# Retention heads with stored block sums and the next values' first product ahead of the scores; MLP down sums accumulated in SBUF; background jobs further apart

## The chip, the cores and the metric

The kernel runs on one core of one Trainium2 chip. The metric is device time in microseconds. Engine names are those of the profile: PE is TensorE's array, PEld its weight loads, DVE VectorE, ACT ScalarE, POOL GpSimd, SP SyncE, which issues most DMAs.

## The reference

One layer of a hybrid block for 512 tokens of width 1024, in float32. Two branches work on the normalized input; a gated mix of them goes through w_out, and an MLP follows.

```python
xn = rmsnorm(x, n_mix_pre)
qa, ka, va, za, beta_logit, a_dt, qb, kb, vb, gb, gate_a, gate_b = split(xn @ w_in)
# Branch A: causal convolution, silu, gated delta rule in chunks of 64, 8 heads
oa = rmsnorm(chunk_gated_delta_rule(qa, ka, va, beta, g), norm_a) * silu(za)
ya = oa @ w_br_a
# Branch B: 4 retention heads, keys of 256, values of 512
qb, kb = rotary(qb), rotary(kb) * 256 ** -0.5
ob = chunk_retention(qb, kb, vb)
ob = rmsnorm(ob, norm_b) * silu(gb)
yb = ob @ w_br_b
mix = (sigmoid(gate_a) * ya + sigmoid(gate_b) * yb) @ w_out
x = x + rmsnorm(mix, n_mix_post)
ff = square(relu(rmsnorm(x, n_mlp_pre) @ w_up)) @ w_down        # d_ff = 4096
out = x + rmsnorm(ff, n_mlp_post)
```

## The kernel before

**Products.** Every float32 matrix is split into a high part (`whi`, made by ACT at L148) and the rest (`wlo`, made by DVE at L149), and a product is three matmuls: high by high, high by low, low by high (`mm3` at L93 to L95; in block products the loop at L322). A weight tile is 128 x 1024 float32, 512 KB. It is loaded by SP into a buffer named `raw` (L103 straight from a weight matrix, L197 for a block), split, and used by 12 matmuls of 512 columns.

**Seven products.** The large products are done by blocks: two by two blocks of the activations and of the weights, with sums of blocks, need seven block products for eight. They are called "11", "12", "22", "s1" to "s4". The activation sums are made on chip. The weight sums come in two ways. Class `BlockSums` stores them in DRAM: a copy DRAM to DRAM on SP's queue (`copy_block`, L169) puts a block into a DRAM tile `sums`, and an accumulating DMA on POOL's queue (`add_block`, L135) adds another block to it. Where sums are not stored, DVE adds raw tiles (`plus`, in Branch B at L1651).

**The pace of the background.** Copies and adds are jobs of two lists, `trickle` and `later_adds`. `pace` is called at each load as the program is built: if the kernel's own clock, a count of matmul columns, has passed `queued`, one job is put right behind that load, and `queued` grows by `JOB_US` = 7.8 (none in the model's time 860 to 985). Where a sum is wanted before its jobs were placed, `raw` places them at once. There are 140 jobs.

**Branch B.** Head h runs as follows: query and key projections, rotary (L1543 to L1549; the key's high and low parts `kr` at L1548 and L1549), scores in four tiles of 512, 384, 256 and 256 columns, times a decay mask into `sc` (L1583), then values and gates by seven products (`seven`, called by `values_and_gates`), the outputs and their norm. The branch product with w_br_b of head h-1 is a Python generator, `branch_seven`; it is started within head h, behind the keys: "11" and "12" run, then `yield`; then the scores; then "s2", "s1", "s3", "s4", "22". Its activations are `og` (features of the head before), its sums of them `osum` (L1628), made from `upper`; its results are added into `acc` at L1658. The PSUM pool psx has three banks `dl` and one `tr`, the pool psm four banks `mm`.

**MLP.** Four groups: an up projection of 1024 columns (`hn` by w_up, relu and square, rows `r` at L1922), then `seven_down`, a block product in the order "11", "12", "s2", "s1", "s3", "s4", "22" (in the last group "s1" ahead of "s2"). Its results add up in `facc`.

**Order.** Each engine's instructions stand in the order that a list scheduler gives them from program order and `tc.high_priority(n)`: a larger n stands earlier. The block products' matmuls are kept in program order. A load stands on SP when the buffer that it fills has been handed out; there are two raw pools of two buffers in Branch B.

Of the kernel before, what the change touches and what calls it, by code (L numbers as in the profile page):

```python
# [10 lines left out]
F32 = mybir.dt.float32  # L11
# [8 lines left out]
P = 128  # L20
# [8 lines left out]
JOBS_FROM, JOB_US = 70.0, 7.8  # L29
# [34 lines left out]
def hybrid_block_kernel(ctx: ExitStack, tc: tile.TileContext, a: dict, out: bass.AP):  # L64
# [90 lines left out]
    class BlockSums:  # L155


        def __init__(self, src, c1, c2, tag, full=True, kts=4):
# [4 lines left out]
            self.made = (2, 1, 3, 0) if full else (2, 0)  # L163
            self.t = {i: dr.tile([P, kts, 512], F32, tag=f"{tag}{i}", name="sums", bufs=1) for i in self.made}
# [18 lines left out]
        def raw(self, i, ks):  # L183
            while any(job[0] is self for job in trickle):
                copy_block()
            while any(dst is t for dst, *_ in later_adds for t in self.parts):
                add_block()
            return block_raw(self.t[i - 1][:, 2 * ks : 2 * ks + 2, :])
# [4 lines left out]
    def block_raw(block):  # L193
# [8 lines left out]
    ga_sums = BlockSums(w_in, OFF_GA, OFF_GA + 512, "ga", False)  # L202
    vg_sums, br_sums = [], []
    for h in range(4):
        vg_sums.append(BlockSums(w_in, OFF_VB + h * 512, OFF_GB + h * 512, f"vg{h}", False))
# [45 lines left out]
    def seven(src, c1, c2, sums, product, temp, out):  # L251
# [1257 lines left out]
    with tc.tile_pool(name="pb", bufs=1) as pb_:  # L1509
# [11 lines left out]
        def values_and_gates(sums, c1, c2, g, out1, out2):  # L1521

            def out(th, ch, ps, u=None, op=None):
                for t in range(2):
                    row = 2 * th + t
                    if ch:
                        nc.vector.tensor_tensor(g[:, row, :], ps[t], u[t], op)
# [8 lines left out]
            seven(w_in, c1, c2, sums, token_product(quarters), tmp, out)  # L1536
# [14 lines left out]
        def scores(h, rows):  # L1551
# [42 lines left out]
        def branch_quarters(h, rows):  # L1594
# [47 lines left out]
        def branch_seven(h, xq, upper):  # L1642
# [6 lines left out]
            def plus(dst, other):  # L1649
                with tc.high_priority(SUM_PRIO):  # L1650
# [483 lines left out]
```

## Time and profile before

| what | number |
|---|---|
| median of 3 runs | 1344.77 us (1341.4, 1344.77, 1345.39) |
| the profiled execution | 1343.75 us, its span 1341.9 us, mean granted clock 0.997 |
| instructions in the span | 17580, of them 6555 matmuls and 6555 weight loads |

By stage (us from the span's start, busy time of each engine):

| stage | stretch | length | PE | DVE | ACT | POOL | DMA share |
|---|---|---|---|---|---|---|---|
| Branch A | 0 to 470 | 470 | 460.38 | 328.49 | 251.81 | 44.79 | 0.59 |
| Branch B head 0, gate A | 470 to 600 | 130 | 128.76 | 104.14 | 56.19 | 12.35 | 0.85 |
| head 1 | 600 to 698 | 98 | 95.50 | 77.47 | 52.09 | 4.00 | 0.59 |
| head 2 | 698 to 795 | 97 | 93.54 | 81.86 | 45.27 | 5.11 | 0.60 |
| head 3 | 795 to 893 | 98 | 94.80 | 84.38 | 47.29 | 0.00 | 0.42 |
| gate B, mix, w_out | 893 to 1000 | 107 | 105.61 | 83.88 | 51.69 | 3.27 | 0.46 |
| MLP | 1000 to 1342 | 342 | 330.43 | 212.36 | 180.94 | 27.01 | 0.76 |

How to read it: a stage in which PE's busy time is nearly the length is bound by TensorE. Length less PE busy is TensorE's idle time: 2.5 to 3.5 us in each of heads 1 to 3, 11.6 us in the MLP (its end among it), 9.6 us in Branch A. The busy time of an instruction that waits inside its predecessor's shadow is modelled, so start to start distances say more than durations where instructions follow each other closely.

### The profile page before, as it was taken

How to read it: one execution, taken by the hardware profiler on the slowest of the kernel's cores; microseconds unless marked ns; L12 is line 12 of the kernel's file. 1: busy time of each engine (PE TensorE's matmuls, PEld its weight loads, DVE VectorE, ACT ScalarE, POOL GpSimd, SP SyncE). 2: the span in 40 equal slices, each digit the busy share in tenths (PEclk: the TensorE clock that was granted, in tenths of full speed). 3: DMA queues.
4: the chain of work that ended last, by engine and by line, in shares of the span. 5: the costliest groups of instructions: out<-in, count | busy, mean ns of one | idle time of the engine just before them, and what ended most of it. 6: DMA issues, size and time to landing. Idle time of an engine off the chain costs nothing.

```text
span 1341.9 us, 17580 instructions
## 1 busy us (share of the span) xinstructions
PE 1309.0 (98%) x6555; PEld 1078.0 (80%) x6555; DVE 972.6 (72%) x1620; ACT 685.3 (51%) x1192; POOL 96.5 (7%) x101
## 2 busy tenths in 40 slices
PE   9999999999999999999999999999999999999997
PEld 7888787888788878877877877887888888888786
DVE  6889757476566578879869879878685746648378
ACT  5783556454534424555554453455256636355364
POOL 2201100000100001110000000000002000001001
PEclk9999999999999999999999999999999999999999
DMA  6337843477775477994495563545629887859735
GB/s 191 130 111 185 201 118 79 110 176 195 193 178 142 105 211 156 286 263 118 114 256 105 163 195 89 164 165 168 230 81 226 237 243 184 260 165 238 204 118 133
DMA packets 119156, 231.01 MB, mean 172 GB/s; under 512 B 7254, under 2 KB 39168, under 8 KB 118816
## 3 DMA queue, kind: packets, MB, share of 16 engines
q1 hardware_dynamic: 98176, 179.85, 41.7%
q0 software_dynamic: 18576, 43.69, 20.1%
q10 hardware_dynamic: 2320, 6.36, 1.3%
q8 instruction: 51, 0.84, 0.2%
q14 instruction: 33, 0.27, 0.1%
HBM read 224.61 MB, written 78.66 MB: 226 GB/s over the span
## 4 chain that ended last, share of the span: by engine, by line
PE 72%; DVE 14%; DMA 6%; ACT 5%; issue 2%; DVEq 0%; ACTq 0%; SPq 0%
PE mm L322 16%; PE mm L673 13%; PE dl L322 11%; PE mm L95 7%; PE mm L94 7%; PE mm L93 7%; PE dl L673 5%; DVE wlo L149 4%; DMA raw<-in_w_in_dram 2%; DMA raw<-sums 2%; ACT whi L148 1%; PE tr L402 1%; PE tr L682 1%; DMA raw<-in_w_up_dram 1%; PE mm L637 1%
## 5 line engine op out<-in xcount | busy, mean ns | idle before, releaser
L149 DVE TENSOR_TENSOR wlo<-raw,whi 128x1024 fp32r<-128x1024 f32 x278 | 339.1, 1222 | 192.2 <-ACT whi L148 191.5
L148 ACT CAST whi<-raw 128x1024 fp32r<-128x1024 f32 x278 | 291.9, 1051 | 361.4 <-PE mm L322 77.9
L673 PE MATMUL mm<-actT,whi 128*128 128x512 f32 x448 | 144.5, 403 | 0.0
L322 PE MATMUL mm<-whi,xsum 128*128 128x512 f32 x384 | 120.6, 390 | 0.0
L93 PE MATMUL mm<-hn,whi 128*128 128x512 f32 (+1 forms) x288 | 105.5, 366 | 2.3 <-ACT r L1922 1.2
L95 PE MATMUL mm<-hn,wlo 128*128 128x512 f32 (+1 forms) x288 | 105.5, 366 | 0.5 <-DVE wlo L149 0.5
L94 PE MATMUL mm<-hn,whi 128*128 128x512 f32 (+1 forms) x288 | 105.3, 366 | 0.0
L673 PEld LDWEIGHTS mm<-actT,whi 128*128 128x128 f32 x448 | 80.6, 188 | 14.7
L673 PE MATMUL mm<-actT,wlo 128*128 128x512 f32 x224 | 87.7, 392 | 0.0
L322 PEld LDWEIGHTS mm<-whi,xsum 128*128 128x128 f32 x384 | 72.0, 188 | 14.7
L322 PE MATMUL mm<-wlo,xsum 128*128 128x512 f32 x192 | 74.9, 390 | 0.0
L322 PE MATMUL dl<-whi,ffq 128*128 128x512 f32 x224 | 71.2, 389 | 0.0
L93 PEld LDWEIGHTS mm<-hn,whi 128*128 128x128 f32 x288 | 54.3, 189 | 11.6 <-ACT whi L148 1.5
L673 PE MATMUL mm<-whi,og 128*128 128x512 f32 x192 | 62.3, 397 | 0.0
L95 PEld LDWEIGHTS mm<-hn,wlo 128*128 128x128 f32 x288 | 54.3, 189 | 9.7 <-DVE wlo L149 1.0
L673 PE MATMUL mm<-whi,actT 128*128 128x512 f32 x176 | 60.3, 404 | 1.0 <-DVE qf L907 1.0
L94 PEld LDWEIGHTS mm<-hn,whi 128*128 128x128 f32 x288 | 54.3, 189 | 8.7
L322 PE MATMUL dl<-whi,actT 128*128 128x512 f32 x192 | 61.1, 389 | 0.0
L322 PE MATMUL mm<-whi,ffq 128*128 128x512 f32 x192 | 60.9, 389 | 0.0
L1927 DVE TENSOR_TENSOR ffq<-r,ffq 128x512 fp32r<-128x512 f32 (+1 forms) x64 | 39.1, 621 | 28.1 <-ACT ffq L1927 27.9
L135 POOL DMA_DIRECT2D sums<-in_w_in_dram x28 | 32.7, 1167 | 339.3 <-DMA sums<-in_w_in_dram 339.3
L93 PE MATMUL mm<-actT,whi 128*128 128x512 f32 x128 | 51.8, 405 | 0.0
(428 smaller groups left out, 2865.8 us busy)
## 6 DMA issues: line engine op xcount, KB each, us to landing
raw<-in_w_in_dram SPq DMA_DIRECT2D x95, 512.0 KB, 4.8
raw<-sums SPq DMA_DIRECT2D x70, 512.0 KB, 4.6
raw<-in_w_up_dram SPq DMA_DIRECT2D x36, 512.0 KB, 6.5
sums<-in_w_in_dram SPq DMA_DIRECT2D x32, 512.0 KB, 5.7
sums<-in_w_down_dram SPq DMA_DIRECT2D x32, 512.0 KB, 5.9
sums<-in_w_in_dram POOLq DMA_DIRECT2D x28, 512.0 KB, 7.5
raw<-in_w_down_dram SPq DMA_DIRECT2D x24, 512.0 KB, 4.9
sums<-sums POOLq DMA_DIRECT2D x20, 512.0 KB, 8.3
```

What stands on the lines that cost most here:

```text
L93: nc.tensor.matmul(ps, lh, rh, start=first, stop=False)
L94: nc.tensor.matmul(ps, lh, rl, start=False, stop=False)
L95: nc.tensor.matmul(ps, ll, rh, start=False, stop=last)
L135: tc.keep_in_program_order(nc.gpsimd.dma_start(dst, src, accum_op=ALU.add))
L148: nc.scalar.copy(hi[:, :n], raw[:, :n])
L149: nc.vector.tensor_tensor(lo[:, :n], raw[:, :n], hi[:, :n], ALU.subtract)
L322: m = nc.tensor.matmul(pss[t], lhs[i // 2], rhs[i % 2], start=first and k + i == 0, stop=k + i == kts + 1, skip_group_check=not first,)
L402: nc.tensor.transpose(ps, src, ident)
L637: pin(nc.tensor.matmul(first_keys[f][:, 256:512], ws[w][:, kk, :], xs[x][:, 2 * j + kk, 256:512], start=False, stop=kk == 1 and i == 2, sk ...
L673: m = tc.keep_in_program_order(nc.tensor.matmul(*args, **kwargs))
L682: tc.keep_in_program_order(nc.tensor.transpose(ps, src, ident if by is None else by))
L1927: return nc.scalar.copy(dst[0], r), nc.vector.tensor_tensor(dst[1], r, dst[0], ALU.subtract)
```

## The change

Four parts.

1. *Branch B's block sums are stored.* `br_sums` now makes all four sums in DRAM (`made=(2, 1, 3, 0)`, two tiles fewer than a full one since kts is 2); `branch_seven` loads them, and its DVE additions at L1651 are gone. The first two results are added into `acc` at priority 0 for 400, and the bank of "s1" is taken from psm for psx.
2. *A product ahead of the scores.* `seven` becomes a generator that yields after "11"; a new generator `values(h)` holds it. For heads 1 to 3, `scores` calls `next(vals)` behind the branch's "12", so that the 24 matmuls of the next values' "11" (into two `dl` banks) stand ahead of the scores. The score tiles alternate between a `dl` bank and the `tr` bank. Transposes go at priority 70 for 100.
3. *Down sums grow in SBUF, groups 0 to 2.* Two pairs of sum tiles stand in the slots tagged "ym". u is loaded with block 11 and used for "11"; a POOL DMA then adds the stored sum t[2], and u is used for "s2"; another adds block 21 (`first[3]`), and u is used for "22". v is loaded with block 12, block 11 is added, and it is used for "s1". "12", "s3" and "s4" load as before. Only one sum of four is stored in DRAM for these groups. Group 3 stays as it was.
4. *Jobs are 9.4 us apart* for 7.8; there are 116.

The core of the diff:

```diff
-JOBS_FROM, JOB_US = 70.0, 7.8
+JOBS_FROM, JOB_US = 70.0, 9.4
...
+            self.made = made
+            self.t = {i: dr.tile([P, 4, 512], F32, tag=f"{tag}{i}", name="sums", bufs=1) for i in self.made}
...
+        def grown(self, pool, tag):
+            def halves(w):
+                return [w[:, 2 * ks : 2 * ks + 2, :] for ks in range(2)]
+            def tiles(src):
+                return [block_raw(w, pool.tile([P, 1024], F32, tag=tag, name="sum", bufs=4)) for w in halves(src)]
+            def plus(raws, src):
+                for raw, w in zip(raws, halves(src)):
+                    nc.gpsimd.dma_start(raw.rearrange("p (k c) -> p k c", k=2), w, accum_op=ALU.add)
+            return tiles, plus
...
+    def block_raw(block, raw=None):
         n = next(loads)
         pool, tag = raw_pools[n % len(raw_pools)]
-        raw = pool.tile([P, 1024], F32, tag=tag, name="raw", bufs=2)
+        if raw is None:
+            raw = pool.tile([P, 1024], F32, tag=tag, name="raw", bufs=2)
...
-            br_sums.append(BlockSums(w_br[1][4 * h * P : 4 * (h + 1) * P, :], 0, 512, f"br{h}", False, 2))
-    gb_sums = BlockSums(w_in, OFF_GBR, OFF_GBR + 512, "gb", False)
-    down_sums = [BlockSums(w_down[grp * D : (grp + 1) * D, :], 0, 512, f"dn{grp}") for grp in range(4)]
+            br_sums.append(BlockSums(w_br[1][4 * h * P : 4 * (h + 1) * P, :], 0, 512, f"br{h}", kts=2))
...
+    down_sums = [
+        BlockSums(w_down[grp * D : (grp + 1) * D, :], 0, 512, f"dn{grp}", (2,) if grp < 3 else (2, 1, 3, 0))
+        for grp in range(4)
+    ]
...
-        p1, u3 = [temp("p1") for _ in range(2)], [temp("u3") for _ in range(2)]
-        x, y = raws(sums.first_raw, 1), raws(sums.raw, 3)
+        x = raws(sums.first_raw, 1)
         a = bank(psx)
         times(a, "11", x, True)
+        yield
+        p1, u3 = [temp("p1") for _ in range(2)], [temp("u3") for _ in range(2)]
+        y = raws(sums.raw, 3)
...
             else:
                 branch = branch_seven(h - 1, *parts)
                 next(branch)
+                next(vals)
             scs = []
             sall = pb_.tile([P, 2560], F32R, tag="s", name="s")
             done = 0
             for i in range(4):
                 t0 = min(i * P, 256)
                 n = T - t0
-                ps = psx.tile([P, T], F32, tag="dl", name="dl", bufs=3)
+                if h and i % 2:
+                    ps = psx.tile([P, T], F32, tag="tr", name="tr", bufs=1)
+                else:
+                    ps = psx.tile([P, T], F32, tag="dl", name="dl", bufs=3)
...
-                with tc.high_priority(100):
+                with tc.high_priority(70):
...
-            x, y = sums.first_raw(1, 0), sums.raw(3, 0)
             a = bank(psm)
-            times(a, "11", x, True)
-            add(0, 0, a, new=True)
-            plus(x, y)
-            v = sums.first_raw(3, 0)
+            times(a, "11", sums.first_raw(1, 0), True)
+            add(0, 0, a, new=True, prio=0)
             b = bank(psm)
-            times(b, "12", v, True)
-            add(0, 0, b)
+            times(b, "12", sums.first_raw(3, 0), True)
+            add(0, 0, b, prio=0)
             branch_sums(xq, upper)
             yield
-            plus(v, x)
-            times(a, "s2", x, False)
+            times(a, "s2", sums.raw(2, 0), False)
             add(0, 1, a, ALU.subtract, new=True)
-            w = sums.raw(1, 0)
-            c = bank(psx)
-            times(c, "s1", w, True)
+            c = bank(psm)
+            times(c, "s1", sums.raw(1, 0), True)
             add(1, 1, c, new=True)
-            times(a, "s3", y, False)
+            times(a, "s3", sums.raw(3, 0), False)
             add(1, 1, a, ALU.subtract)
-            w = sums.first_raw(2, 0)
-            times(c, "s4", w, False)
+            times(c, "s4", sums.first_raw(2, 0), False)
             add(0, 1, c)
-            times(a, "22", v, False)
+            times(a, "22", sums.raw(4, 0), False)
             add(1, 0, a, new=True)
...
+            parts = values_and_gates(vg_sums[h], OFF_VB + h * 512, OFF_GB + h * 512, gs, value, gate)
+            next(parts)
+            yield
+            pairs = [[pb_.tile([P, 2, T], F32R, tag=f"vr{i}{x}", name="vr") for x in "ab"] for i in range(2)]
+            vs += [[w[:, t, :] for w in pair for t in range(2)] for pair in pairs]
+            gs.append(pb_.tile([P, 4, T], F32, tag="kr", name="gs"))
+            for _ in parts:
+                pass
+            yield vs, gs[0]
...
+            vals = values(h)
+            scs = scores(h, rows, vals)
...
+            if not h:
+                next(vals)
+            rows = outputs(scs, *next(vals))
...
+            tiles, plus = sums.grown(pm, "ym")
+            def times(pss, name, raws, first):
+                for ks in range(2):
+                    product(pss, name, ks, split_weights(raws[ks], 1024, 2), first)
...
+            if grp < 3:
+                sums.ready()
+                u = tiles(sums.first[0])
+                v = tiles(sums.w12)
+                plus(v, sums.first[0])
             a = bank(psx)
-            plain(a, "11", 0, 0, True)
+            if grp < 3:
+                times(a, "11", u, True)
+                plus(u, sums.t[2])
+            else:
+                plain(a, "11", 0, 0, True)
...
             def s1():
-                summed(c, "s1", 1, True)
+                if grp < 3:
+                    times(c, "s1", v, True)
+                else:
+                    summed(c, "s1", 1, True)
                 add(1, 1, c, new=True)
 
             def s2():
-                summed(a, "s2", 2, False)
+                if grp < 3:
+                    times(a, "s2", u, False)
+                    plus(u, sums.first[3])
+                else:
+                    summed(a, "s2", 2, False)
                 add(0, 1, a, ALU.subtract, new=True)
...
-                summed(a, "22", 4, False)
+                times(a, "22", u, False)
```

What it does to the order of instructions. First TensorE in head 2, at the end of the branch product "12" (`mm<-whi,og`), where the scores (`dl<-qr,kr`) begin. Before:

```order
L322 MATMUL mm<-whi,og 128x512
L93 MATMUL dl<-qr,kr 128x512
L94 MATMUL dl<-qr,kr 128x512
L93 MATMUL dl<-qr,kr 128x384
L94 MATMUL dl<-qr,kr 128x384
L93 MATMUL dl<-qr,kr 128x256
L94 MATMUL dl<-qr,kr 128x256
L95 MATMUL dl<-qr,kr 128x512
L93 MATMUL dl<-qr,kr 128x512
L94 MATMUL dl<-qr,kr 128x512
```

and after (the middle of the 24 matmuls of "11", `dl<-whi,actT`, is left out):

```order
L345 MATMUL mm<-whi,og 128x512
L345 MATMUL dl<-whi,actT 128x512
L345 MATMUL dl<-wlo,actT 128x512
...
L345 MATMUL dl<-wlo,actT 128x512
L345 MATMUL dl<-whi,actT 128x512
L93 MATMUL dl<-qr,kr 128x512
L94 MATMUL dl<-qr,kr 128x512
...
L95 MATMUL dl<-qr,kr 128x512
L93 MATMUL tr<-qr,kr 128x384
L94 MATMUL tr<-qr,kr 128x384
```

Before, the scores follow "12" at once, and the 512, 384 and 256 column tiles are interleaved over the three dl banks; now "11" of the next values stands between, and the score tiles come one after the other, on dl and tr in turn.

VectorE in head 2, from the rotary sums (`ro`, L1545) to the first additions into `osum`. Before:

```order
L1545 TENSOR_TENSOR ro<-ro 128x512
L149 TENSOR_TENSOR wlo<-raw,whi 128x1024
L1546 TENSOR_TENSOR ro<-ro 128x512
L1549 TENSOR_TENSOR kr<-ro,kr 128x512
L1634 SCALAR_TENSOR_TENSOR upper<-upper,og 128x2x256
L1549 TENSOR_TENSOR kr<-ro,kr 128x512
L1636 TENSOR_TENSOR upper<-upper 128x2x256
L1583 TENSOR_TENSOR sc<-dl,dec 128x512
L1583 TENSOR_TENSOR sc<-dl,dec 128x384
L1583 TENSOR_TENSOR sc<-dl,dec 128x256
L1583 TENSOR_TENSOR sc<-dl,dec 128x128
L1628 TENSOR_TENSOR osum<-upper,osum 128x512 x2
```

and after (`kr` is now L1572, `sc` L1610, `osum` L1655, `acc` L1681):

```order
L1572 TENSOR_TENSOR kr<-ro,kr 128x512 x2
L1681 TENSOR_TENSOR acc<-acc,mm 128x512
L149 TENSOR_TENSOR wlo<-raw,whi 128x1024
L1681 TENSOR_TENSOR acc<-acc,mm 128x512 x2
L149 TENSOR_TENSOR wlo<-raw,whi 128x1024
L1681 TENSOR_TENSOR acc<-acc,mm 128x512
L1655 TENSOR_TENSOR osum<-upper,osum 128x512
L1666 TENSOR_TENSOR upper<-upper,og 128x2x256
L1610 TENSOR_TENSOR sc<-dl,dec 128x512
L149 TENSOR_TENSOR wlo<-raw,whi 128x1024
L1610 TENSOR_TENSOR sc<-tr,dec 128x384
L1610 TENSOR_TENSOR sc<-dl,dec 128x256
```

Before, the four score reads stand together behind the keys and ahead of `osum`; now both low halves of the keys, two splits, four additions into `acc` and one into `osum` stand ahead of the first score read, and a split stands between the first and the second.

SyncE at the end of the down product of group 1 and the begin of the next up projection. Before:

```order
L103 DMA raw_9932<-in_w_down_dram 128x2x512
L103 DMA raw_9951<-in_w_down_dram 128x2x512
L197 DMA raw_9971<-sums_103 128x1024
L197 DMA raw_9989<-sums_103 128x1024
L169 DMA sums_109<-in_w_down_dram 128x2x512
L103 DMA raw_10020<-in_w_up_dram 128x2x512
L103 DMA raw_10050<-in_w_up_dram 128x2x512
```

and after:

```order
L103 DMA raw_9923<-in_w_down_dram 128x2x512
L103 DMA raw_9941<-in_w_down_dram 128x2x512
L169 DMA sums_108<-in_w_down_dram 128x2x512
L215 DMA sum_10312<-in_w_down_dram 128x2x512
L215 DMA sum_10315<-in_w_down_dram 128x2x512
L103 DMA raw_10006<-in_w_up_dram 128x2x512
L169 DMA sums_108<-in_w_down_dram 128x2x512
L103 DMA raw_10037<-in_w_up_dram 128x2x512
```

The two loads of the stored sum for "22" (`raw<-sums`) are gone; the loads into the next group's u (`sum<-`, L215) stand ahead of w_up, and the jobs lie differently.

POOL's queue in the MLP, the piece of the difference around the second and third groups' sums:

```order
-L135 DMA sums<-sums 128x1024 x2
+L206 DMA sum<-in_w_down_dram 128x2x512 x2
+L206 DMA sum<-sums 128x1024 x2
+L206 DMA sum<-in_w_down_dram 128x2x512 x2
+L135 DMA sums<-in_w_down_dram 128x2x512 x4
+L206 DMA sum<-in_w_down_dram 128x2x512 x2
+L206 DMA sum<-sums 128x1024 x2
+L206 DMA sum<-in_w_down_dram 128x2x512 x2
 L135 DMA sums<-in_w_down_dram 128x2x512
-L135 DMA sums<-sums 128x1024 x2
-L135 DMA sums<-in_w_down_dram 128x2x512 x3
```

The adds between DRAM tiles (`sums<-`, L135) are mostly gone, and adds into SBUF (`sum<-`, L206) stand in their place.

More of the change, by code (lines that the diff above doesn't have):

```diff
@@ L1534, in out @@
                         out1(row, v)
-            seven(w_in, c1, c2, sums, token_product(quarters), tmp, out)
+            return seven(w_in, c1, c2, sums, token_product(quarters), tmp, out)
         def rotary(pss, dst):
@@ L1647, in times, with add @@
                 product(pss, x, 0, split_weights(raw, 1024, 2), first)
-            def plus(dst, other):
-                with tc.high_priority(SUM_PRIO):
-                    nc.vector.tensor_tensor(dst, other, dst, ALU.add)
-            def add(th, ch, parts, op=ALU.add, new=False):
-                with tc.high_priority(400):
+            def add(th, ch, parts, op=ALU.add, new=False, prio=400):
+                with tc.high_priority(prio):
                     for t in range(2):
@@ L1691, in features, with values @@
             return gated_features(rows, lambda f: nb[:, 4 * h + f : 4 * h + f + 1])
-        def outputs(h, scs):
-            pairs = [[pb_.tile([P, 2, T], F32R, tag=f"vr{i}{x}", name="vr") for x in "ab"] for i in range(2)]
-            vs = [[w[:, t, :] for w in pair for t in range(2)] for pair in pairs]
-            gs = pb_.tile([P, 4, T], F32, tag="kr", name="gs")
+        def values(h):
+            vs, gs = [], []
             def value(t, p):
@@ L1737, in out @@
                     gated(2 * th + t, ch, src)
-            seven(w_in, off, off + 512, sums, token_product(quarters), tmp, out)
+            for _ in seven(w_in, off, off + 512, sums, token_product(quarters), tmp, out):
+                pass
         rows = None
         for h in range(4):
-            scs = scores(h, rows)
+            vals = values(h)
+            scs = scores(h, rows, vals)
             if h == 0:
```

28 lines of the change are left out of this document (14 added, 14 removed).

## The prediction

> **What bounds the kernel now.** I read the page first, then TensorE's waits, then the timeline of the places where it waits, and last the queues that feed those places. The page says that the array is nearly always busy:
>
> ```profile
> span 1341.9 us, 17580 instructions
> PE 1309.0 (98%) x6555; PEld 1078.0 (80%) x6555; DVE 972.6 (72%) x1620; ACT 685.3 (51%) x1192; POOL 96.5 (7%) x101
> ```
>
> The change leaves the number and shapes of the matmuls as they are, so all it can win is idle time of TensorE, about 33 us in all, and all it can lose is new idle time. In the list of who waited for whom (total us, times, longest) these rows of TensorE belong to places that the diff touches:
>
> ```profile
> PE dl L93 <- ACT kr L1548: 4.3, 2, 2.2
> PE dl L95 <- DVE kr L1549: 1.5, 3, 0.8
> PE mm L93 <- ACT r L1922: 1.2, 1, 1.2
> PE mm L322 <- DVE osum L1628: 1.0, 2, 0.5
> PE dl L322 <- DVE osum L1628: 0.5, 1, 0.5
> PE mm L95 <- DVE wlo L149: 0.5, 1, 0.5
> ```
>
> kr and osum are the keys and the summed features in Branch B's heads 1 to 3; r and wlo at L149 belong to the MLP stage. The timeline of TensorE (start, duration, engine, line, operands, idle time before) shows what a head loses. In each of the next three pieces the first row is the last matmul of the branch product "12", the last row the first matmul of "s2", and between them lie only the 24 score matmuls.
>
> ```profile
> 626.10 0.39 PE L322 MATMUL mm<-whi,og 128*128 128x512 f32 x1
> 626.32 0.39 PE L93 MATMUL dl<-qr,kr 128*128 128x512 f32 x1
> 626.55 0.39 PE L94 MATMUL dl<-qr,kr 128*128 128x512 f32 x1
> 626.77 0.33 PE L93 MATMUL dl<-qr,kr 128*128 128x384 f32 x1
> 626.95 0.34 PE L94 MATMUL dl<-qr,kr 128*128 128x384 f32 x1
> ...
> 632.02 0.28 PE L95 MATMUL dl<-qr,kr 128*128 128x256 f32 x1
> 632.14 0.39 PE L322 MATMUL mm<-whi,osum 128*128 128x512 f32 x1
> ```
>
> ```profile
> 721.18 0.39 PE L322 MATMUL mm<-whi,og 128*128 128x512 f32 x1
> 723.74 0.50 PE L93 MATMUL dl<-qr,kr 128*128 128x512 f32 x1 [2.17 <-ACT kr L1548]
> ...
> 730.06 0.40 PE L322 MATMUL mm<-whi,osum 128*128 128x512 f32 x1
> ```
>
> ```profile
> 818.94 0.39 PE L322 MATMUL mm<-whi,og 128*128 128x512 f32 x1
> ...
> 826.51 0.39 PE L322 MATMUL mm<-whi,osum 128*128 128x512 f32 x1
> ```
>
> Start to start, a score matmul takes 0.23 us at 512 columns, 0.18 at 384 and 0.12 at 256: 6 x 0.23 + 6 x 0.18 + 12 x 0.12 = 3.9 us, and 0.2 for the last matmul of "12". The three stretches are 6.04, 8.88 and 7.57 us, so 1.9 + 4.8 + 3.5 = 10.2 us are lost. The osum waits (1.0 + 0.5 us) come just behind. Together the heads lose 11.7 us. The reason is VectorE's queue:
>
> ```profile
> 701.00:727.00 26.00, 23.46 (x105) 18.80 (x104) 25.14 (x35) 10.88 (x15) 2.49 (x3) 0.96 0.59 134
> 716.17 0.69 DVE L1543 TENSOR_TENSOR ro<-mm,rope 128x512 f32<-128x512 f32 x1 [0.19 <-PE mm L95]
> 716.77 0.68 DVE L1544 TENSOR_TENSOR ro<-mm,rope 128x512 f32<-128x512 f32 x1
> 717.37 1.22 DVE L149 TENSOR_TENSOR wlo<-raw,whi 128x1024 fp32r<-128x1024 f32 x1
> 718.50 1.28 DVE L1658 TENSOR_TENSOR acc<-acc,mm 128x512 f32<-128x512 f32 x2
> ...
> 725.90 0.68 DVE L1549 TENSOR_TENSOR kr<-ro,kr 128x512 fp32r<-128x512 f32 x1
> ...
> 728.50 1.48 DVE L1583 TENSOR_TENSOR sc<-dl,dec 128x512 f32<-128x512 f32 x3 [1.32 <-PE dl L95]
> ```
>
> In head 2 VectorE is busy for 25.14 of the 26 us up to 727 (the window row gives the stretch, then PE, PEld, DVE, ACT and POOL busy, clock and DMA). The key product ends just before 716.17, and the second low half of the keys starts only at 725.90, whereas TensorE has been out of work since 721.4.
>
> **The change, part by part.**
>
> *The 24 matmuls of the next values' "11" ahead of the scores.* They need two weight tiles straight from w_in and no keys, so they run 2 x 2.72 = 5.4 us (24 x 0.227) while VectorE finishes the keys. In the new order VectorE does, from 716.17 on, two rotary products, a split, two rotary sums, a split and the two low halves: six at 0.60 start to start and two splits at 1.13, 5.9 us, done near 722.2. The scores start at 721.4 + 5.4 = 726.8: the keys are 4.6 us early. The cover needs the two x tiles split in time; their slots in the ring of three are free at 716 and 718.7, their products start at 721.4 and 724.1, so that holds by about 3 us. osum is now built long before "s2". All 11.7 us are covered. On SP the two loads move ahead of the branch's remaining loads; what they displace is priced below.
>
> *Scores on two alternating banks.* Two of the three dl banks now hold "11", so the third score tile waits until the first is read, the fourth until the second is. VectorE's order is now first score read (0.60, as its other 128x512 operations take from start to start), a split (1.13), second score read (0.5: three take 1.48 in the last row above). With 0.2 us from a matmul's end to the read (0.19 in the row of 716.17) and, I assume, as much from a read to the matmul that it lets go, the fourth tile can start 0.2 + 0.6 + 1.13 + 0.5 + 0.2 = 2.6 us after the first tile's end; the second and third take 6 x 0.18 + 6 x 0.12 = 1.8 us. New wait: 0.8 us a head, 2.4 us in all (0 if the split slips behind, 2 us a head if more stands ahead of it).
>
> *Branch B's sums stored.* VectorE loses six operations of this row, two a head, in the stretch where it is full; that is part of the 5.9 us above and not counted again:
>
> ```profile
> L1651 DVE TENSOR_TENSOR raw<-raw x6: 1212/1216/1217, 613.2 to 812.5; 128x1024 f32<-128x1024 f32 x6
> ```
>
> In their place stand two more loads a head, and two copies and two adds a head in the background. The two x tiles keep two of four raw buffers until the values' second product, so seven tiles (five of the branch, two of the values) go through the other two. Their price is the time to landing of the loads of L197 in this stage, 16 of them from stored sums:
>
> ```profile
> L197 SPq DMA_DIRECT2D raw<-sums x16: 338/339/494, 605.3 to 855.7; - x16
> DMA to landing us min/median/max: 3.3/3.9/12.9
> ```
>
> A buffer turns round in 3.9 us of load and 2.4 of split, 6.3 us for two products' worth of 5.4 us, but the scores and "11" give 9 us of head start, and the last of the seven comes about 1 to 2 us before its product. At the median: nothing. One load at the maximum of 12.9 us would cost some 7 us. The two first adds of a head now go late in the queue (priority 0, c in the other PSUM pool): they need VectorE before "s1", 10 us later, so nothing.
>
> *Down sums in SBUF, groups 0 to 2.* Of 14 raw loads a group 10 remain (four into the sum tiles), of 16 background transfers 4, and six accumulating DMAs are new, on POOL's queue. PE, ACT and DVE do the same work. TensorE's two long waits in this stage are these:
>
> ```profile
> 1026.56 0.50 PE L93 MATMUL mm<-hn,whi 128*128 128x512 f32 x1 [1.25 <-ACT r L1922]
> 1250.99 0.50 PE L93 MATMUL mm<-hn,whi 128*128 128x512 f32 x1 [1.09 <-ACT whi L148]
> ```
>
> At 1250 it is the load of w_up, issued at 1236.5, that lands late:
>
> ```profile
> L103 SPq DMA_DIRECT2D raw<-in_w_up_dram x4: 367/376/389, 1236.5 to 1245.8; - x4
> DMA to landing us min/median/max: 12.6/13.3/14.1
> ```
>
> In the new order "22" takes its weights from a sum tile, so w_up's first loads take the buffers of "s3" and not of "s4", two tiles or 5.4 us earlier, and fewer adds run beside them. The next group's u loads stand ahead of them on SP, but take the slots of v, free since "s1" was split, so they hold nothing up. I take both waits as gone: 1.25 + 1.09 + 0.5 (wlo) = 2.8 us (0 if loads stay as slow).
>
> The new wait: u is split for "11", then POOL adds the stored sum to it, then it is split for "s2". The rows are of the down product of group 1, the second tile's low half in "11" and the high half in "s2":
>
> ```profile
> 1131.11 1.23 DVE L149 TENSOR_TENSOR wlo<-raw,whi 128x1024 fp32r<-128x1024 f32 x1 [0.48 <-ACT whi L148]
> 1141.18 1.05 ACT L148 CAST whi<-raw 128x1024 fp32r<-128x1024 f32 x1 [1.71 <-PE mm L322]
> ```
>
> From 1131.11 + 1.23 to 1141.18 there are 8.8 us for the add (the first tile has more). No add into SBUF is in this trace. Its bounds are a plain POOL load into SBUF, and the adds in DRAM of this stage (the last row is of all 23 adds of L135 between 1001 and 1255):
>
> ```profile
> acc<-in_x_dram POOLq DMA_DIRECT2D x4, 512.0 KB, 3.7
> L135 POOL DMA_DIRECT2D sums<-in_w_down_dram x11: 1135/1172/2373, 1011.6 to 1249.0; - x11
> DMA to landing us min/median/max: 5.3/9.6/22.0
> ```
>
> 3.7 us costs nothing, 22.0 us costs 13.2 us a group. I take the median 9.6, the nearest row in place and size: 0.8 us late, 2.4 us over three groups. Behind the waiting split on ACT stand all later splits, so TensorE waits the same time. The other adds (v before "11", u for "22") have over 20 us. The Trainium skill, "DMA: Bandwidth & Descriptors", section "Anatomy of one DMA — SWDGE (gpsimd) path", fits a DMA of this queue at 2.0 us plus bytes over 436e3; for 512 KB that is 3.2 us, an estimate by that page, and by it these 2.4 us would be nothing. The trace's adds are two to three times as long, so I keep the row.
>
> *The rest.* Jobs 9.4 us apart: 116 for 140, and where a sum would come late its last adds are put on POOL's queue at once; they wait only for copies issued long before. Under 1 us either way, I take 0. The transposes' priority of 70 leaves TensorE's order as it was, and the values' temporaries, taken after "11", have the same slots: 0.
>
> Sum: -11.7 + 2.4 - 2.8 + 2.4 = -9.7 us.
>
> **The rivals.** *The wait in the heads moves.* VectorE was full before; if the x splits, the score reads or the seven tiles on two buffers come late, each head gives back some 2 us more: 6 us, 1341. For it speaks the 1 to 2 us of slack; against it the landing of 3.9.
>
> *Given back in the MLP.* An add of about 12 us costs 3.2 a group, 9.5 in all, 7 more than I took: with the waits of 2.8 left as well the time is within 4 us of the old one, about 1345.
>
> *Slower: the add before "s2" decides.* All else as forecast, the kernel is slower by over 4 us (0.3%, about what a measurement can tell from no change) when the three waits sum to 2.4 + 9.7 + 4 = 16 us, that is when the add takes 8.8 + 5.4 = 14.2 us; at 16 us it is 1354. Such adds are in the trace (up to 22.0), where several ran at once beside loads. The Trainium skill's page "DMA: Bandwidth & Descriptors", section "Queues, rings and completion order", has the engines take turns between queues that have work, which fits; against it, only two adds are in flight here, and fewer copies run beside them.
>
> **How the numbers follow.** The profiled run took 1343.75 us with its span of 1341.9; the median of the three runs shown is 1344.77, 1.0 higher. From the median: 1344.77 - 9.7 = 1335. Chances: the forecast 0.61 (1330 with no wait at the adds and half of the score waits, to 1338); heads giving back 0.16 (1338 to 1341.5); given back in the MLP 0.14; slower 0.09. The range 1330 to 1341.5 holds the first two. Faster 0.77, same 0.14, slower 0.09.
>
> **What would show it.** After the change the kr and osum waits should be gone from TensorE's waits, the scores should follow a product into dl without a gap, a wait of 0.8 us for sc should stand before the fourth score tile, and VectorE should have six operations fewer. In the MLP the waits at the group borders should be gone, and ACT's split of u for "s2" should show whether it waited for a DMA. I am wrong if that wait exceeds 3 us a group, if raw loads are what the branch's last tiles wait for, or if kr is still late.

## The result, and the profile after

| | before | changed |
|---|---|---|
| median | 1343.09 us (4 runs, 1340.29 to 1345.39) | 1332.05 us (4 runs, 1330.75 to 1332.55) |
| ratio of the changed kernel to before | | 0.9917, 95% interval 0.9893 to 0.9941 |
| profiled execution, span | 1343.75 us, 1341.9 us | 1332.26 us, 1330.3 us |

The kernel became 11.0 us faster; 9.7 were forecast, with 1335 as the time, and 1332.05 lies in the range. The two first rows of the page of the changed kernel show the same matmuls, six VectorE operations fewer, six more DMAs on POOL:

```profile
span 1330.3 us, 17581 instructions
PE 1306.2 (98%) x6555; PEld 1076.8 (81%) x6555; DVE 965.7 (73%) x1614; ACT 684.8 (51%) x1192; POOL 104.8 (8%) x107
```

Of TensorE's waits (total us, times, longest) those for kr, osum, r and whi at the group borders are gone. These are new:

```profile
PE dl L345 <- DVE wlo L149: 3.2, 2, 1.6
PE tr L93 <- DVE sc L1610: 2.5, 3, 1.0
PE mm L345 <- DVE wlo L149: 0.6, 1, 0.6
```

Where the time went is read by setting the start of the same matmul in both traces side by side:

| up to | before, us | changed, us | shift | won in the stage | forecast |
|---|---|---|---|---|---|
| a product of head 0 | 573.49 | 570.04 | -3.45 | 3.45 | 0 |
| w_br_b of head 3, behind the heads | 929.67 | 922.01 | -7.66 | 4.2 | 9.3 |
| last up projection's start | 1252.25 | 1241.08 | -11.17 | 3.5 | 0.4 |

So the total came out near the forecast by luck, through misses that cancel: the heads won less than half of what was forecast, and two places where next to nothing was forecast won 7 us.

TensorE in head 2 (start, duration, engine, line, operands, idle time before). "11" follows "12" at once, and the scores follow "11" at once; then one wait, ahead of the fourth score tile:

```profile
716.88 0.39 PE L345 MATMUL mm<-whi,og 128*128 128x512 f32 x1
717.11 0.39 PE L345 MATMUL dl<-whi,actT 128*128 128x512 f32 x1
...
722.32 0.39 PE L345 MATMUL dl<-whi,actT 128*128 128x512 f32 x1
722.55 0.39 PE L93 MATMUL dl<-qr,kr 128*128 128x512 f32 x1
...
726.63 0.39 PE L93 MATMUL tr<-qr,kr 128*128 128x256 f32 x1 [0.79 <-DVE sc L1610]
...
727.46 0.40 PE L345 MATMUL mm<-whi,osum 128*128 128x512 f32 x1
```

From 716.88 to 727.46 are 10.6 us, of which 9.5 are matmuls (0.2 + 5.4 + 3.9). VectorE at the same place shows why the fourth tile waits, a split between the first read and the second, which frees the tr bank:

```profile
724.11 0.69 DVE L1610 TENSOR_TENSOR sc<-dl,dec 128x512 f32<-128x512 f32 x1
724.89 1.22 DVE L149 TENSOR_TENSOR wlo<-raw,whi 128x1024 fp32r<-128x1024 f32 x1
726.03 0.55 DVE L1610 TENSOR_TENSOR sc<-tr,dec 128x384 f32<-128x384 f32 x1
```

The other new wait is in the values' "12", second tile (TensorE, then ACT, then SP's queue with time and count of DMAs):

```profile
756.93 0.50 PE L345 MATMUL dl<-wlo,actT 128*128 128x512 f32 x1 [1.60 <-DVE wlo L149]
749.91 2.00 ACT L148 CAST whi<-raw 128x1024 fp32r<-128x1024 f32 x2 [2.62 <-DMA raw<-in_w_in_dram]
741.55 4.99 SPq L215 DMA_DIRECT2D raw<-in_w_in_dram  x2
```

Between the second high half and its low half VectorE has other work, and the low half comes only here (the first of two):

```profile
755.66 2.49 DVE L149 TENSOR_TENSOR wlo<-raw,whi 128x1024 fp32r<-128x1024 f32 x2
```

The loads for "12" at 741.55 and 746.15 wait for the buffers of x, which come free when VectorE has added x to y. They are issued 10.4 and 8.5 us ahead of their products; in the kernel before it was 12.2 and 12.5 us. ACT stands idle until 749.91 for the second one, whose high half is done at 751.9; from 752.14 to 755.66 VectorE does four sums and a block addition that stand ahead of the low half, and TensorE waits for that. All idle time of ACT ahead of a split that waits for such a load between 600 and 860, of the kernel before and of the changed one:

```profile
  ACT whi L148: 5.3, 2
```

```profile
  ACT whi L148: 35.1, 15
DMA to landing us min/median/max: 3.5/4.1/11.5
```

The loads themselves are no slower (median 4.1 us, 3.9 before): they start later.

In the MLP the accumulating DMAs into SBUF take less than the 9.6 us at which the prediction took them from adds in DRAM. The list of DMA issues (count, KB, median us to landing):

```profile
sum<-sums POOLq DMA_DIRECT2D x6, 512.0 KB, 5.7
sum<-in_w_down_dram POOLq DMA_DIRECT2D x12, 512.0 KB, 7.1
```

ACT's two splits of u for "s2" in group 1 wait for TensorE to free a weight buffer, and for no DMA:

```profile
1126.59 1.05 ACT L148 CAST whi<-sum 128x1024 fp32r<-128x1024 f32 x1 [0.70 <-PE dl L345]
1129.31 1.06 ACT L148 CAST whi<-sum 128x1024 fp32r<-128x1024 f32 x1 [0.48 <-PE mm L345]
```

### The profile page after: what moved, and what is told of

It reads as the page before. It is cut to its first block, busy times and chain, and to the rows that moved or that the text cites. A ratio compares the mean times of both kernels' runs of the same rounds, so it can differ in the third digit from the quotient of the medians.

```text
span 1330.3 us, 17581 instructions
## 1 busy us (share of the span) xinstructions
PE 1306.2 (98%) x6555; PEld 1076.8 (81%) x6555; DVE 965.7 (73%) x1614; ACT 684.8 (51%) x1192; POOL 104.8 (8%) x107
## 4 chain that ended last, share of the span: by engine, by line
PE 75%; DVE 12%; ACT 6%; DMA 4%; issue 2%; ACTq 0%; DVEq 0%
PE mm L696 16%; PE mm L345 15%; PE dl L345 8%; PE mm L94 8%; PE mm L95 8%; PE mm L93 8%; PE dl L696 5%; DVE wlo L149 3%; DMA raw<-sums 2%; ACT whi L148 2%; PE tr L425 1%; PE tr L705 1%; PE dl L93 1%; PE dl L95 1%; PE dl L94 1%
## 5 line engine op out<-in xcount | busy, mean ns | idle before, releaser
L149 DVE TENSOR_TENSOR wlo<-raw,whi 128x1024 fp32r<-128x1024 f32 x254 | 309.4, 1221 | 183.7 <-ACT whi L148 182.5
L148 ACT CAST whi<-raw 128x1024 fp32r<-128x1024 f32 x254 | 266.2, 1051 | 333.1 <-PE mm L696 65.2
L135 POOL DMA_DIRECT2D sums<-in_w_in_dram x28 | 32.6, 1163 | 422.1 <-DMA sums<-in_w_in_dram 422.1
```

The costliest lines, as they stand in the source:

```text
L135: tc.keep_in_program_order(nc.gpsimd.dma_start(dst, src, accum_op=ALU.add))
L148: nc.scalar.copy(hi[:, :n], raw[:, :n])
L149: nc.vector.tensor_tensor(lo[:, :n], raw[:, :n], hi[:, :n], ALU.subtract)
```

## The experiments

Every time below is a median, with the ratio to runs of the kernel before on the same chip. The medians of the kernel before in the four sets of runs lie between 1343.1 and 1344.7 us, so differences of 1 or 2 us between rows say little.

| kernel | us | ratio, 95% interval |
|---|---|---|
| E1 changed, jobs 7.8 us apart | 1340.26 | 0.9963, 0.9945 to 0.9980 |
| E2 before, jobs 9.4 us apart | 1338.10 | 0.9944, 0.9925 to 0.9962 |
| E3 changed, no sums in SBUF | 1347.66 | 1.0020, 1.0003 to 1.0036 |
| E4 changed, heads as before | 1336.47 | 0.9934, 0.9916 to 0.9952 |
| E5 changed, jobs 10.4 us apart | 1343.45 | 0.9990, 0.9976 to 1.0004 |
| E6 before, sums in SBUF | 1341.49 | 0.9974, 0.9959 to 0.9989 |
| E7 changed, score reads first | 1332.92 | 0.9920, 0.9903 to 0.9936 |
| E8 changed, own slot for x | 1327.79 | 0.9883, 0.9865 to 0.9902 |
| E9 E8 with another bank | 1323.31 | 0.9836, 0.9810 to 0.9862 |
| E10 changed, add twice | 1348.09 | 1.0021, 1.0002 to 1.0041 |
| E11 changed, jobs 8.6 us apart | 1335.37 | 0.9932, 0.9906 to 0.9958 |
| E12 changed, only stored sums in the heads | 1331.43 | 0.9904, 0.9878 to 0.9930 |

The traces (one execution each) divide the time at the same three matmuls as above, in us:

| kernel | jobs apart | to the product of head 0 | to w_br_b of head 3 | to the last up projection |
|---|---|---|---|---|
| before | 7.8 | 573.49 | 356.18 | 322.58 |
| E2 before, wider pace | 9.4 | 570.08 | 355.63 | 320.53 |
| E6 before, sums in SBUF | 7.8 | 576.17 | 356.25 | 318.94 |
| E4 changed, old heads | 9.4 | 569.17 | 355.58 | 319.01 |
| E1 changed, old pace | 7.8 | 577.43 | 352.86 | 319.00 |
| changed | 9.4 | 570.04 | 351.97 | 319.07 |
| E12 changed, product not moved | 9.4 | 568.91 | 352.73 | 319.11 |
| E8 changed, own slot | 9.4 | 569.53 | 347.67 | 319.07 |
| E9 changed, own slot and bank | 9.4 | 569.65 | 343.87 | 318.98 |

The first stretch goes with the pace, the second with the heads, the third with the sums in SBUF and, by 2 us, with the pace.

### The pace: E1, E2, E5, E11

```diff
-JOBS_FROM, JOB_US = 70.0, 9.4
+JOBS_FROM, JOB_US = 70.0, 7.8    # E1; in E5 10.4, in E11 8.6; E2 is before with 9.4
```

What was expected of E1:

> The changed kernel with jobs 7.8 us apart again. Theory: the 3.45 us that the changed kernel won before the first reordered head (Branch A and head 0) come from the pace alone, so this kernel takes 3 us more than the changed one, about 1335, and TensorE's wait of 1.6 us for vt near 345 is back. Rival: those 3.45 us are a difference between single executions (the three runs before spread over 4 us); then it stays at 1332 within 1 us.

What was expected of E2:

> The kernel before with jobs 9.4 us apart and nothing else. Theory: Branch A and head 0 win 3 us, the time falls to about 1340. Rival: no difference from before, 1343 within 1 us; or slower, if jobs that come too late are placed in a row at the MLP.

What was expected of E5:

> The changed kernel with jobs 10.4 us apart. Theory: jobs beside the weight loads cost time where a load lands late (7.8 us apart cost 8 us against 9.4), so a further step wins a little more before the MLP, 1 to 3 us, about 1330, as long as the sums are still made in time; if sums come late, a wait of several us for whi or wlo shows at one place and the time is over 1335. Rival: the 8 us came from where single jobs happened to lie, then the step may go either way by some 2 us.

What was expected of E11:

> The changed kernel with jobs 8.6 us apart. If the time depends on how many jobs run beside loads, it lies between 1332 (9.4) and 1340 (7.8), about 1336. If it depends on where single jobs meet single loads, it may lie anywhere from 1330 to 1342, and the place that loses is another than at 7.8.

E1 is 8.2 us slower than the changed kernel, E2 6.5 us faster than the one before, each more than twice the 3 us expected. By these two runs the pace, which the prediction set at nothing, is the largest single part. One place shows how it acts, Branch A near 345. ACT and POOL of the kernel before, then ACT of the changed one:

```profile
337.37 1.16 POOL L135 DMA_DIRECT2D sums<-in_w_in_dram  x1 [14.71 <-DMA sums<-in_w_in_dram]
...
345.69 1.04 ACT L148 CAST whi<-raw 128x1024 fp32r<-128x1024 f32 x1 [5.15 <-DMA raw<-in_w_in_dram]
346.64 0.83 ACT L1375 ACTIVATE vt<-dl,eg 128x256 f32<-128x256 f32 x2
```

```profile
341.31 1.05 ACT L148 CAST whi<-raw 128x1024 fp32r<-128x1024 f32 x1 [1.76 <-PE dl L696]
342.26 0.84 ACT L1398 ACTIVATE vt<-dl,eg 128x256 f32<-128x256 f32 x2
```

Before, an add of the background starts at 337.37 just ahead of two weight loads (338.15 and 341.83), which land after 7.4 and 5.0 us; ACT waits 5.15 us for the first, `vt` stands behind that split in ACT's queue, and TensorE waits for `vt`. After, POOL's next add starts at 343.05, the load of 337.24 lands in 4.0 us, and ACT waits for none. In E1 and E6 too an add (at 338.27 and 337.96) starts just ahead of that load, which lands after 8.5 and 8.1 us; in E2 there is none, and it lands in 3.7 us. That the add slows the load is read from these five traces; no run moved this one add alone. The wait of TensorE in the kernel before, and in E1:

```profile
PE dl L673 <- ACT vt L1375: 1.6, 1, 1.6
```

```profile
PE dl L696 <- ACT vt L1398: 2.8, 1, 2.8
```

All three kernels with 7.8 (before, E1, E6 with 2.45 us) have it; the changed kernel and E2 have not. But wider is not better: at 10.4 the time is back at 1343.45. Two waits in E5 make most of that:

```profile
PE dl L93 <- ACT osq L1745: 3.4, 2, 3.0
PE mm L93 <- ACT r L1951: 2.9, 1, 2.9
```

Ahead of the first, POOL's queue holds three adds closer together than the pace:

```profile
862.09 1.14 POOL L135 DMA_DIRECT2D sums<-in_w_in_dram  x1 [18.35 <-DMA sums<-in_w_in_dram]
867.38 1.14 POOL L135 DMA_DIRECT2D sums<-in_w_in_dram  x1 [4.16 <-DMA sums<-in_w_in_dram]
873.56 1.14 POOL L135 DMA_DIRECT2D sums<-in_w_in_dram  x1 [5.04 <-DVE wlo L149]
```

They were placed at once, since the sums for gate B, the stage behind head 3, were not made when they were wanted; a weight load issued at 864.57 lands after 11.2 us, ACT stands idle 3.94 us for it, and the gates (gs), which VectorE's product o and then osq need, stand behind that split. Of the four paces tried with the changed kernel 9.4 is the best: 1340.3 at 7.8, 1335.4 at 8.6, 1332.05 at 9.4, 1343.5 at 10.4. E11's profiled execution took 1340.17 and was the slowest of its six, so its places say little about the 1335.4. Whether the number of jobs or the places where they meet loads counts more stays open: the three narrower paces lie in order, but the waits are at single places in every trace, and the kernels with 7.8 reach the product of head 0 up to 4 us apart (573.49, 576.17, 577.43), though up to there, by the edits, only the jobs differ.

### The sums in SBUF: E3, E6, E10

```diff
 # E3
-            if grp < 3:
+            if False:                 # the four uses; made=(2, 1, 3, 0) for all groups
 # E10
                 plus(u, sums.t[2])
+                plus(u, sums.t[2])
```

E6 is the kernel of E4, described below, with jobs 7.8 us apart.

What was expected of E3:

> The changed kernel with the down sums of groups 0 to 2 stored in DRAM as before, jobs 9.4 us apart (152 jobs). Theory from the two traces, by which the MLP won 3.5 us: about 1335.5, with the waits for r and whi at the borders of the groups back. By the prediction's terms for the MLP (2.8 won, 2.4 lost) 1332.5. Over 1338 would say that jobs placed too late cost more than the sums in SBUF win.

What was expected of E6:

> The kernel before with the sums in SBUF for groups 0 to 2 and nothing else, jobs 7.8 us apart. Prediction's terms for the MLP: 0.4 won (2.8 won, 2.4 lost), 1344. Theory from the traces (the MLP won 3.5 us and no sum was waited for): 3 us won, about 1341.5. Rival: sums in SBUF are worth nothing by themselves and only make the wider pace possible, 1344.5.

What was expected of E10:

> The changed kernel in which POOL adds the stored sum to u twice, so that two adds of 5.7 us stand one after the other between the splits for 11 and for s2 (the result of s2 then has weights that hold that sum once too often). By the prediction's slack of 8.8 us the second tile's split comes 2.6 to 3.5 us late in each of three groups: 8 to 10 us slower than the changed kernel, 1340 to 1342, more if the array's clock falls after each wait. Rival: the slack is larger than the prediction has it, and the time stays at 1332 to 1335.

E6 wins 3.2 us on before: the waits at the group borders are gone there and nothing in the MLP takes their place, as the theory had it. E3 is 15.6 us slower than the changed kernel, over four times what was expected, and most of it is one wait, for a stored sum of the first down group:

```profile
PE mm L345 <- ACT whi L148: 13.6, 1, 13.6
```

With 152 jobs 9.4 us apart that sum is not made in time. The kernel before, with 140 jobs, stood the same pace (E2); with the branch's stored sums added, it takes the sums in SBUF to bring the jobs down to a number that this pace can place. The waits for r and whi at the borders of the groups were expected back in E3 and did not come (though TensorE's stand of 13.6 us may hide them), and in E2 the one for whi is gone by the pace alone (that for r stays, 1.3 us). So what ends these waits is not one thing.

In E10 TensorE waits in each of the three groups for the split of u (2.57, 2.70 and 1.33 us):

```profile
PE dl L345 <- ACT whi L148: 6.6, 3, 2.7
```

The first two are what was expected, two adds of 5.7 us less a slack of 8.8, but by luck, since neither number holds. The adds took 6.8 us (the median of twelve), and with the time in POOL's queue the second tile's split started 18.1 us after its low half in "11" had ended (1033.95):

```profile
1052.06 1.04 ACT L148 CAST whi<-sum 128x1024 fp32r<-128x1024 f32 x1 [7.02 <-DMA sum<-sums]
```

And the slack is longer than the prediction has it. The splits of that group in the kernel before stand in the order of their products: 1119.15 and 1124.75 for "11", 1130.03 and 1132.97 for "12", 1135.69 and 1138.41 for "s2". So the row of 1131.11 that the prediction takes for the second tile of "11" belongs to the first of "12", and 1141.18 to the first of "s1". The right rows are these:

```profile
1125.96 1.22 DVE L149 TENSOR_TENSOR wlo<-raw,whi 128x1024 fp32r<-128x1024 f32 x1
...
1138.41 1.06 ACT L148 CAST whi<-raw 128x1024 fp32r<-128x1024 f32 x1 [0.48 <-PE mm L322]
```

From the end of the first (1125.96 + 1.22 = 1127.18) to 1138.41 are 11.2 us, and TensorE comes to that tile only at 1143.65, so its split, which takes 1.05 us, may start as late as 1142.6 without a wait: the slack is 15.4 us. In the three groups of E10 18.1, 18.2 and 16.9 us less 15.4 give 2.7, 2.8 and 1.5, close to what TensorE waited.

E10 is 16 us slower than the changed kernel, not 8 to 10. The rest is the array's clock, and the low half of the second tile, for which TensorE waits 0.76 us more each time; the windows (stretch, PE, PEld, DVE, ACT, POOL busy, clock, DMA share, GB/s) show the clock, before the first of these waits and behind it:

```profile
1045.00:1050.00 5.00, 5.00 (x24) 4.14 (x23) 2.00 (x4) 0.04 (x1) 1.23 (x2) 1.00 0.93 166
...
1053.10:1057.00 3.90, 3.08 (x7) 2.31 (x8) 3.86 (x5) 2.46 (x5) 2.34 (x4) 0.56 0.16 15
1057.00:1060.00 3.00, 3.00 (x8) 2.35 (x8) 1.43 (x2) 1.04 (x2) 2.36 (x3) 0.50 1.09 172
```

### The heads: E4, E7, E8, E9, E12

```diff
 # E4: branch_seven, scores and outputs of the kernel before, br_sums with (2, 0)
 # E12: stored sums kept; next(vals) behind the scores, score tiles on dl
 # E7
-                with tc.high_priority(400):   # score read
+                with tc.high_priority(900):
 # E8
+            x.append(block_raw(sums.first[1][:, 2:4, :], pb_.tile([P, 1024], F32, tag="xw", name="xw")))
 # (room: tag "tm" with 7 buffers for 8, "dec" with 1 for 2)
 # E9: E8 and
+                if h and i == 3:
+                    ps = psm.tile([P, T], F32, tag="mm", name="mm")
```

What was expected of E4:

> The changed kernel with Branch B as before (two stored sums, DVE additions, scores ahead of the next values' first product, score tiles on dl), with the sums in SBUF and jobs 9.4 us apart. By the two traces, in which heads 1 to 3 won 4.2 us, it takes 1336; by the prediction's terms (11.7 won, 2.4 lost) 1341.

What was expected of E7:

> The changed kernel with VectorE's score reads at priority 900 for 400, so that no split stands between the first and the second. Theory: the wait for sc before the fourth score tile (0.66, 0.79 and 1.04 us) falls to under 0.3 us a head, 2 us won, about 1330. Rival: the split that is put behind is late in its place, and nothing is won, 1332.

What was expected of E8:

> The changed kernel with a slot of its own for the second x tile of values and gates, so that three raw buffers for two are left while the branch's tail runs (the room comes from one temporary of eight and from the second mask buffer). Theory: the waits for wlo in the values of heads 1 to 3 (0.6, 1.6 and 1.6 us) come from the two held buffers; they fall by half or more, 2 to 4 us won, about 1329. Rival: they come from the order on VectorE (four sums of the products ahead of the low half); then they stay, and the time with them, 1332.

What was expected of E9:

> The kernel with the own slot for one x tile (1327.8), and the fourth score tile in a bank of the mm pool, which the branch product 12 has left, for the tr bank. Theory: the waits for sc (0.8, 0.9 and 1.3 us) go, and 2.5 to 3 us are won, about 1325. Rival: the branch product s1, which takes the same bank next, now waits for the score read, and nothing is won, 1328.

What was expected of E12:

> The changed kernel with the next values' first product behind the scores and the score tiles on dl, as before; the branch's sums are stored, the down sums in SBUF, jobs 9.4 us apart. Theory: six VectorE operations of 1.2 us less in a full queue shorten the wait for kr by a part only; between the kernel with the old heads (1336.5) and that less 4 us, I take 1334. Rival: moving the product is what counts, 1336.5.

E4 is 4.4 us slower than the changed kernel, as the two traces said, and not 9.3. Its waits are those of the kernel before:

```profile
PE dl L93 <- ACT kr L1571: 4.3, 2, 2.2
PE dl L95 <- DVE kr L1572: 1.5, 3, 0.8
PE mm L345 <- DVE osum L1654: 1.0, 2, 0.5
```

E12 is the surprise: with the sums stored and the product left where it was, the kernel is as fast as the changed one (1331.43 and 1332.05, with overlapping runs). No wait for kr is left. The trace points less to the six additions than to another part of the edit, the first additions into `acc` at priority 0. In E4, as before, four of them (2.4 us) stand between the key product and the keys' last low half (`kr`, 721.41); in E12 they stand behind it:

```profile
716.67 1.28 DVE L1684 TENSOR_TENSOR acc<-acc,mm 128x512 f32<-128x512 f32 x2
```

```profile
713.67 1.28 DVE L1572 TENSOR_TENSOR kr<-ro,kr 128x512 fp32r<-128x512 f32 x2
...
718.38 3.22 DVE L1680 TENSOR_TENSOR acc<-acc,mm 128x512 f32<-128x512 f32 x5
```

The additions of raw tiles stand ahead of that stretch: at 711.68 in E4, as at 716.17 in the kernel before, VectorE has caught up and waits for the key product. No run changed the priority alone. What is left in E12 is one row, behind the five additions of 718.38:

```profile
PE mm L345 <- DVE osum L1654: 5.2, 2, 2.6
```

The moved product takes this wait away and brings those for sc and wlo. E8 and E9 take these two away. With a slot of its own for one x tile no wait for wlo is left in the values (4.3 us won on the changed kernel), only that for sc, a little longer:

```profile
PE tr L93 <- DVE sc L1613: 3.0, 3, 1.3
```

With the fourth score tile in the bank that "12" has left, that goes too (4.5 us more), and head 2 runs from "11" through all 24 score matmuls into "s2" in 3.86 us for the scores, the first of which and the first matmul of "s2" are these:

```profile
720.07 0.39 PE L93 MATMUL dl<-qr,kr 128*128 128x512 f32 x1
...
723.93 0.40 PE L347 MATMUL mm<-whi,osum 128*128 128x512 f32 x1
```

E9 is the fastest kernel here, 1323.31 us, 21 us less than before. From E4 to E9 the heads' stretch falls by 11.7 us in the traces (13.2 between the medians), and 11.7 is what the prediction took for the heads' idle time. E7 told nothing: the priority left VectorE's order as it was, so it is one more measurement of the changed kernel, 0.9 us from the first.

## Why the prediction was right, and where it was wrong

- **The product as a cover for the keys: the signs came, the cause is not shown.** No wait for kr or osum is left in the changed kernel's heads, and the scores follow "11" without a gap. But E12 has no wait for kr either, without the move. Its trace points to the late additions into `acc`, for which the prediction took nothing; that they do it alone was not tried. What the move itself takes away, from E12 to the changed kernel, is the wait for osum.
- **The scores' banks: right in place and size.** 0.8 us a head was the term, 0.66, 0.79 and 1.04 were measured, for the reason given (a split between the first read and the second); E9 takes it away with a bank.
- **"At the median: nothing" for the seven tiles on two buffers: wrong.** The loads took what was assumed (4.1 us); the head start of 9 us was counted for seven tiles and did not reach the two behind them, the tiles of "12", which load into the buffers that x leaves. 3.8 us were lost there, and E8 wins 4.3 back. This is the rival in which the wait in the heads moves, which had 6 us.
- **The add ahead of "s2": 2.4 us forecast, none measured, and two numbers of the term wrong.** 9.6 us was taken from adds between DRAM tiles; into SBUF the stored sum's add took 5.7 us (5.4 to 6.5), nearer to the plain load's 3.7. The estimate by the Trainium skill's page "DMA: Bandwidth & Descriptors", section "Anatomy of one DMA — SWDGE (gpsimd) path", 3.2 us, was below the 5.7 measured, but gave the right term. And the slack of 8.8 us was read from rows of the wrong tiles, and a late split was taken for a wait of TensorE at once; it is 15.4 us, by the rows of before and by E10. An add of 9.6 us would have cost nothing, and the prices and thresholds of the two rivals that count from 8.8 are 6.6 us too early.
- **The waits at the group borders: right in size,** 2.8 us forecast and gone; E6 measured 3.2. Which of the two reasons given (earlier loads, fewer adds) ends them is not shown, and the pace alone ends part of them (E2).
- **"The rest", the pace at 0: wrong, and the largest miss.** By E1 and E2 it is worth 8.2 and 6.5 us, and 3.4 us of it stand ahead of everything else that was changed. The prediction weighed only jobs placed too late and not what each job does to the weight loads beside it, although the profile of before had the wait for vt and the 5.15 us of ACT ahead of it.

The sum was right by luck: the heads fell short by 5.1 us, while the MLP and the stages ahead of the heads won 6.6 us more than forecast. The parts don't add everywhere: in the third stretch of the table the pace alone wins 2.1 us, the sums in SBUF alone 3.6, and both together (E4) 3.6.

## What to carry to other kernels

A product moved ahead of a wait must bring its own buffers and banks: what it holds longer is paid by the loads and reads behind it, and here the move was worth nothing until an x slot and a PSUM bank were added, then 8 us (E12 to E9; the slot and the bank without the move were not run). Background copies have a price at the loads that they run beside, and a price in bunches when they come too late; a pace that 116 and 140 jobs stood was too wide for 152, so time the pace and the number of jobs together. When a forecast comes out right, compare it stage by stage before believing its terms.

## What the runs showed of the hardware

A wait of TensorE can cost more than itself. In the fourteen traces, leaving out the start of the program, 17 waits of TensorE were 2.17 us or longer. Within 4.9 us of the begin of 13 of them the granted clock fell to 0.50 and stayed there for 3.4 us, which costs 1.7 us (longer for those of 2.57, 3.00 and 13.6 us); behind the other four, the longest of them 2.76 us in E1, it stayed at 1.00. Of 23 waits between 1.22 and 1.65 us only one, of 1.43 us in E11, had such a fall behind it. So the length of the wait alone does not decide. In E12 the two waits for osum, 5.2 us, each have a fall behind them, 3.4 us more; together that is 8.6 us, and the heads' stretch of E9, which has no such wait, is 8.9 us shorter than E12's. The Trainium skill, "TensorE: Matmul & The Clock Gate", section "Part 1: The HAM clock gate (the "warmup" mystery)", has the array fall to half rate after an idle window of about 3.4 us; the half rate agrees, but here waits of 2.17 us were enough in some places, and once 1.43 us.

An accumulating DMA of 512 KB into SBUF took 5.7 us where the stored sum was read and 7.1 where the weight matrix was, against 12.0 for adds of the same stage into DRAM (`sums<-in_w_down_dram` on POOL's queue of the changed kernel); which part of the difference is the target and which the load beside them was not tried.
